# A whole gate unit's slot given back behind its own products, and each expert's case bit taken at its gather

## The chip, the core and the metric

One core of a Trainium2 chip runs the whole program in one launch. The metric is the device time of one execution in microseconds (us); lower is better.

## What is computed

Two layers of a decoder trunk on 256 tokens of width 1024, in fp32. Each layer has a mixer (a gated MLP beside gated linear attention) and a feed-forward part; layer 0's is a dense SwiGLU, layer 1's a mixture of 8 SwiGLU experts of which each token uses 2:

```
logits = t @ w_router
top_val, top_idx = lax.top_k(logits, 2)
gates = sum(one_hot(top_idx) * softmax(top_val))
for e in range(8):
    out = out + gates[:, e:e+1] * ((silu(t @ e_gate[e]) * (t @ e_up[e])) @ e_down[e])
```

The expert weights are 1024 x 3584 (gate, up) and 3584 x 1024 (down), 352 MB in all, and are read once. The change lies in this last stage.

## The kernel before

**Units and slots.** Weights come in units of 1 MB (128 x 2048 fp32). `W`, a `Stream` (lines 127 to 230), holds the list of all units in the order of their use, the plan. A unit passes through slots of SBUF, 18 in this stage. `load` takes a slot and issues the DMA on SP's queue into raw tile r. `converting` takes two more slots and splits r into h (rounded to fp32r, by ACT, line 271) and l (the rest r - h, by DVE, line 272); DVE's l is the last reader of r, whose slot is then given back. PE multiplies with h and l. `drop` gives back l's slot of a unit in an even place, `free` the rest. Slots given back go to the end of the list `idle`, and whoever needs one takes the first. Whoever writes a slot waits for the last reader of what was in it.

**Whole units.** The first unit of every gate block but the very first (line 795, `whole=(0,)`) isn't split: PE takes r as it is, with the input in full fp32 (`self.xw`, line 1050), in twice as many passes of PE; `parts` then holds `(r, None)`. There are 31 such units.

**Order.** The program is written out by Python in the order of PE's products. Before each product step `tick` (line 253) advances the time `W.now` by one, lets side tasks go on, and calls `pump` (line 198): it loads while `len(idle) > 1 + max(0, freed + reserve - split)`, and converts the next unit of the plan where two slots are idle and the unit is due within `lead` ticks (12 here). ACT, DVE and SP each work through their instructions in this order.

**Experts.** An expert's 3584 hidden columns go in groups of 512, 1024, 1024 and 1024 (the last expert in the reverse order). In the main loop (lines 1215 to 1240) a group's gate product (4 units of 1 MB, or 2 for 512 columns), its up product and the down product of the group before follow each other; this is a group's cycle, e.g. 48 ticks. `Expert.product` (line 1035) works by pairs of units. In the narrow case, an expert with at most 64 tokens, the two halves of the input share a pass, and a unit takes two passes; in the wide case it takes three. The third passes, and the last second pass of a pair, run in `last_passes` under a branch (`cases`, line 964: a register holds the expert's bit of a mask; every engine carries the branch). The slots of both units of a pair are given back behind it (`held`). `gated` copies or applies Silu to the gate product (sge), `finish` copies the up product (upe) and, 13 and 17 ticks on, makes the transposed hidden ("hide": PE's folding matmuls with line 1108, ACT line 1110, DVE lines 1111 to 1113). `scatter` adds an expert's output to acc (line 1169). `gather_from_scratch` prepares the next expert's input (exh, exl, xw).

**Registers.** `routing` loads the mask of wide experts into a register of PE, ACT and DVE (line 905) and takes all eight bits out of it at once (line 908).

Numbers of units below are their places in the plan: 290 is ('eu', 5, 2, 1), the second up unit of expert 5's third group; h290, l290 and r290 are its tiles.

Of the kernel before, what the change touches and what calls it, by code (L numbers as in the profile page):

```python
# [39 lines left out]
def trunk(ctx: ExitStack, tc: tile.TileContext, x, w_in, gm_ws, gm_bs, gm_ln_g, gm_ln_b, gla_wa2, gla_ba,  # L40
          gla_norm_g, w_out, ln_mix_g, ln_mix_b, ffn_g, ffn_u, ffn_d, router_w, exp_g, exp_u, exp_d,
          ln_ffn_g, ln_ffn_b, out):
    nc = tc.nc
# [14 lines left out]
    def s2(name, dt=F32, shape=(P, 512)):  # L58
        return act.tile(list(shape), dt, tag="s2", name=name, bufs=6)
# [10 lines left out]
    def psy(name, shape=(P, 512), dt=F32):  # L70
        return ps_y.tile(list(shape), dt, tag="y", name=name)
# [55 lines left out]
    class Stream:  # L127
# [98 lines left out]
        def free(self, key):  # L226
            assert self.index[key] == self.freed, (key, self.index[key], self.freed)
            self.parts.pop(self.freed)
            idle.extend(self.held.pop(self.freed))
            self.freed += 1  # L230
# [596 lines left out]
    def moe(xT, ready, consts):  # L827
# [6 lines left out]
        def logits(tb):  # L834
            pl = psy(f"lg{tb}", (2 * NE, P))
            thin(pl, rw, xT[tb], NE)
            lT = s2(f"lT{tb}", F32, (2 * NE, P))
            nc.scalar.activation(lT, pl, AF.Copy)
            lTs.append(lT)
# [6 lines left out]
        def first_max(src, nm):  # L846
            m = const.tile([P, 2, 1], F32, name=f"m{nm}")
            nc.vector.tensor_reduce(m, src, axis=AX.X, op=ALU.max)
            q = const.tile([P, 2, NE], F32, name=f"q{nm}")
            nc.vector.tensor_tensor(q, src, bc(m), op=ALU.is_equal)  # L850
            nc.vector.tensor_tensor(q, q, pri_b, op=ALU.mult)
            r = const.tile([P, 2, 1], F32, name=f"r{nm}")
            nc.vector.tensor_reduce(r, q, axis=AX.X, op=ALU.max)
            nc.vector.tensor_tensor(q, q, bc(r), op=ALU.is_equal)
            return m, q
# [10 lines left out]
        def routing():  # L866
            yield 2
            logits(0)
            yield 8
            ready.finish()  # L870
            logits(1)
            yield 2
            for tb in range(2):
                nc.tensor.matmul(plt[:, tb, :], lTs[tb], pair, start=True, stop=True)
            nc.vector.tensor_copy(lg, plt)
            m1, oh1 = first_max(lg, "1")
            lg2 = const.tile([P, 2, NE], F32, name="lg2")
            nc.vector.scalar_tensor_tensor(lg2, oh1, -3.0e38, lg, op0=ALU.mult, op1=ALU.add)
            m2, oh2 = first_max(lg2, "2")
            nc.vector.tensor_tensor(sel, oh1, oh2, op=ALU.add)  # L880
            W.pump(1, 100)
            ut = s2("ut")[:, 0:P]
            nc.gpsimd.memset(ut, 1.0)
            nc.gpsimd.affine_select(ut, ut, pattern=[[1, P]], compare_op=ALU.is_ge, fill=0.0, base=-1,
                                    channel_multiplier=-1)
            yield 6

            pr = psy("pr", (P, 2, NE))
            nc.tensor.matmul(pr[:, 0, :], ut, sel[:, 0, :], start=True, stop=True)
            nc.tensor.matmul(pr[:, 1, :], ut, sel[:, 1, :], start=True, stop=False)  # L890
            nc.tensor.matmul(pr[:, 1, :], ones, sel[:, 0, :], start=False, stop=True)
            pc = psy("pc", (P, NE))
            for tb in range(2):
                nc.tensor.matmul(pc, ones, sel[:, tb, :], start=tb == 0, stop=tb == 1)
            nc.vector.scalar_tensor_tensor(rk, pr, 1.0, sel, op0=ALU.add, op1=ALU.mult)
            nc.vector.tensor_scalar(rk, rk, -1.0, None, op0=ALU.add)
            nc.vector.tensor_scalar(small, pc, HALF + 0.5, float(-HALF), op0=ALU.is_lt, op1=ALU.mult)

            bits = const.tile([P, NE], F32, name="bits")
            msum = const.tile([P, 1], F32, name="msum")  # L900
            nc.vector.scalar_tensor_tensor(bits, pc, HALF + 0.5, powers, op0=ALU.is_gt, op1=ALU.mult)
            nc.vector.tensor_reduce(msum, bits, axis=AX.X, op=ALU.add)
            nc.vector.tensor_copy(mask_i, msum)
            experts[0].one_hot()
            mask = nc.values_load(mask_i[0:1, 0:1], engines=[ET.PE, ET.Activation, ET.DVE], min_val=0,
                                  max_val=2 ** NE - 1)
            for e in range(NE):
                experts[e].wide = nc.snap(mask & 2 ** e)
            W.pump(1, 100)
            yield 1  # L910
            yield from experts[0].gather()

            cnt = const.tile([P, 1], F32, name="cnt")
            nc.vector.tensor_reduce(cnt, pc, axis=AX.X, op=ALU.max)
            nc.vector.tensor_copy(cnt_i, cnt)
            W.hold = False
            yield 60

            w12 = const.tile([P, 2, 2], F32, name="w12")
            dl = const.tile([P, 2], F32, name="dl")  # L920
            nc.vector.tensor_tensor(dl, m2[:, :, 0], m1[:, :, 0], op=ALU.subtract)
            nc.gpsimd.tensor_tensor(dl, ecst, dl, op=ALU.pow)
            nc.vector.tensor_scalar(w12[:, 0, :], dl, 1.0, None, op0=ALU.add)
            nc.vector.reciprocal(w12[:, 0, :], w12[:, 0, :])
            nc.vector.tensor_tensor(w12[:, 1, :], dl, w12[:, 0, :], op=ALU.mult)
            for tb in range(2):
                nc.vector.tensor_scalar(gates[:, tb, :], oh1[:, tb, :], w12[:, 0, tb:tb + 1], None, op0=ALU.mult)
                nc.vector.scalar_tensor_tensor(gates[:, tb, :], oh2[:, tb, :], w12[:, 1, tb:tb + 1], gates[:, tb, :],
                                               op0=ALU.mult, op1=ALU.add)
                nc.vector.tensor_scalar(acc[tb], xf[tb], ALPHA, None, op0=ALU.mult)  # L930
# [20 lines left out]
        class Expert:  # L951
# [6 lines left out]

            def __init__(self, nm, rank, gate, fewer=None):
                self.nm, self.rank, self.gate, self.fewer = nm, rank, gate, fewer  # L960
                self.wide = None
                self.hT = {}

            def cases(self, few, many):
# [36 lines left out]
                                         stop=tb == 1)  # L1001

            def gather_from_scratch(self):
                self.one_hot()
                yield 4
                yield from self.gather()
# [28 lines left out]
            def product(self, units, n, nm):  # L1035

                xh, xl = self.x
                nb = n // 512
                p = [psw(f"{nm}{b}") for b in range(nb)]
                kk = 2048 // n  # L1040
                held, rest, last = [], [], []
                for u, ((wh, wl), free, drop) in enumerate(units):
                    held.append(free)
                    for j in range(kk):
                        k = kk * u + j
                        for b in range(nb):
                            s = slice(b * 512, b * 512 + 512)
                            tick()
                            if wl is None:
                                nc.tensor.matmul(p[b], self.xw[:, k, :], wh[:, j, s], start=k == 0, stop=False,  # L1050
                                                 skip_group_check=True)
                                continue
                            nc.tensor.matmul(p[b], xh[:, k, :], wh[:, j, s], start=k == 0, stop=False,  # L1053
                                             skip_group_check=True)
                            rest.append((p[b], xl[:, k, :], wh[:, j, s], False))
                            second = p[b], xh[:, k, :], wl[:, j, s], k == KT - 1
                            if k == KT - 1 or (u % 2, j, b) == (1, kk - 1, nb - 1):
                                last.append(second)
                            else:
                                nc.tensor.matmul(*second[0:3], start=False, stop=False, skip_group_check=True)  # L1060
                    if u % 2 == 0:
                        drop()
                    if u % 2 and (nb > 1 or u == 1):
                        self.last_passes(rest, last)
                        for free in held:
                            free()
                        held, rest, last = [], [], []
                return p
# [104 lines left out]
        def stream(keys):  # L1173
            for key in keys:
                yield W.get(key), lambda key=key: W.free(key), lambda key=key: W.drop(key)

        experts = [Expert(str(e), lambda tb, e=e: rk[:, tb, e:e + 1], lambda tb, e=e: gates[:, tb, e:e + 1],
                          small[:, e:e + 1]) for e in range(NE)]
# [222 lines left out]
```

## Time and profile before

| | |
|---|---|
| three runs | 1342.43, 1343.06, 1344.02 us; median 1343.06 |
| the profiled execution | 1342.48 us |
| its span, first to last instruction | 1340.8 us |
| granted TensorE clock, mean over the span | 0.996 |
| DMA moved | 426.35 MB, mean 318 GB/s |

The profile is of one execution. Busy time is that of an engine's instructions; "<-" names whose semaphore ended an idle stretch; a name with q (DVEq, SPq) is that engine's sequencer, and PEld is the weight load of PE. In the timeline equal instructions that follow each other stand in one row with their count, and the bracket is the idle time before the first. The MoE stage takes the time from some 430 us to the end; its first expert's products begin earlier, beside the routing.

### The profile page before, as it was taken

Reading aid. Unit: us, or ns where it says so; the run is one execution under the profiler, and the core shown is the slowest. Engines: PE = TensorE matmul, PEld = TensorE weight load, DVE = VectorE, ACT = ScalarE, POOL = GpSimd, SP = SyncE. Lnnn points to the kernel's source line nnn. Section 1 sums busy time; section 2 is a strip of 40 time slices with the busy share of each in tenths; the row PEclk is TensorE's granted clock in tenths of the full one; section 3 lists DMA queues with packets and bytes.
Section 4 is the critical chain, followed back from the end, with each engine's and each line's share of the span. In section 5 each row is a group of like instructions: output and inputs, shape, how many; then the busy total and the mean of one; then the engine's idle time right before and its main releaser. Section 6 shows DMA issues by size and latency. Waiting matters only on the chain. (4 is left out here: it accounts for less than half of the span.)

```text
span 1340.8 us, 16964 instructions
## 1 busy us (share of the span) xinstructions
PE 1296.5 (97%) x6113; PEld 1024.0 (76%) x6113; DVE 1068.5 (80%) x965; ACT 839.0 (63%) x702; POOL 37.7 (3%) x79
## 2 busy tenths in 40 slices
PE   8999999999998999999999999999999999999996
PEld 7878888888887788777778877776776776777774
DVE  6687544476684887898888789899899989989997
ACT  5653444346342666687756667776777777877783
POOL 1012000000110000000000000000000000000000
PEclk9999999999999999999999999999999999999998
DMA  9636656543484598999999899999999999999993
GB/s 343 256 126 205 240 188 204 203 157 132 159 301 162 222 365 321 392 370 380 408 368 369 320 384 370 389 408 412 408 389 408 409 393 410 407 400 403 412 407 118
DMA packets 118766, 426.35 MB, mean 318 GB/s; under 512 B 8089, under 2 KB 10722, under 8 KB 104578
## 3 DMA queue, kind: packets, MB, share of 16 engines
q1 hardware_dynamic: 117218, 420.61, 81.0%
q0 software_dynamic: 1440, 4.33, 1.1%
q8 instruction: 64, 1.05, 0.3%
q14 instruction: 44, 0.36, 0.1%
HBM read 423.86 MB, written 1.05 MB: 317 GB/s over the span
## 5 line engine op out<-in xcount | busy, mean ns | idle before, releaser
L272 DVE TENSOR_TENSOR l<-r,h 128x2048 fp32r<-128x2048 f32 (+2 forms) x373 | 833.3, 2249 | 134.0 <-ACT h L271 117.6
L271 ACT ACTIVATE h<-r 128x2048 fp32r<-128x2048 f32 (+2 forms) x373 | 685.0, 1881 | 124.1 <-PE bank L1032 39.1
L1137 PE MATMUL bank<-h,che 128*128 128x512 f32 x440 | 174.4, 396 | 0.0
L1053 PE MATMUL eu<-h,exh 128*128 128x512 f32 x440 | 167.5, 389 | 0.0
L1144 PE MATMUL bank<-l,che 128*128 128x512 f32 x377 | 153.3, 407 | 7.0 <-DVEq L969 3.5
L1060 PE MATMUL eu<-l,exh 128*128 128x512 f32 x361 | 141.0, 391 | 0.3 <-DVE l L272 0.3
L1053 PE MATMUL eg<-h,exh 128*128 128x512 f32 x316 | 128.2, 418 | 0.0
L1050 PE MATMUL eg<-r,xw 128*128 128x512 f32 x248 | 114.5, 595 | 0.0
L1144 PEld LDWEIGHTS bank<-l,che 128*128 128x128 f32 x377 | 70.8, 188 | 41.9 <-DVE l L272 17.1
L1053 PEld LDWEIGHTS eu<-h,exh 128*128 128x128 f32 x440 | 82.6, 188 | 16.9
L1137 PEld LDWEIGHTS bank<-h,che 128*128 128x128 f32 x440 | 82.8, 188 | 15.2
L1060 PE MATMUL eg<-l,exh 128*128 128x512 f32 x237 | 92.7, 391 | 0.1
L1060 PEld LDWEIGHTS eu<-l,exh 128*128 128x128 f32 x361 | 67.8, 188 | 15.9 <-DVE l L272 2.1
L1050 PEld LDWEIGHTS eg<-r,xw 128*128 128x128 f32 x248 | 45.2, 190 | 39.6 <-issue 37.8
L266 PE MATMUL f<-h,xhm 128*128 128x512 f32 (+1 forms) x192 | 72.2, 376 | 0.0
L267 PE MATMUL f<-l,xhm 128*128 128x512 f32 (+1 forms) x192 | 71.4, 372 | 0.0
L268 PE MATMUL f<-h,xlm 128*128 128x512 f32 (+1 forms) x192 | 71.4, 372 | 0.0
L1053 PEld LDWEIGHTS eg<-h,exh 128*128 128x128 f32 x316 | 59.5, 188 | 15.4 <-issue 4.1
L1110 ACT ACTIVATE hide<-bank 128x256 f32<-128x256 f32 x42 | 16.1, 384 | 71.7 <-PE bank L1108 71.7
L1060 PEld LDWEIGHTS eg<-l,exh 128*128 128x128 f32 x237 | 44.6, 188 | 12.7 <-issue 3.8
L1075 ACT ACTIVATE sge<-eg 128x512 f32<-128x512 f32 x55 | 30.2, 595 | 36.4 <-PE eg L1032 36.3
L1108 PEld LDWEIGHTS bank<-fold,sge 128*128 128x128 f32 x336 | 46.0, 196 | 5.2 <-issue 2.4
(354 smaller groups left out, 1803.3 us busy)
## 6 DMA issues: line engine op xcount, KB each, us to landing
r<-in_exp_w_gate SPq DMA_DIRECT2D x112, 1024.0 KB, 11.1
r<-in_exp_w_up SPq DMA_DIRECT2D x112, 1024.0 KB, 7.5
r<-in_exp_w_down SPq DMA_DIRECT2D x110, 1024.0 KB, 11.6
r<-in_w_in SPq DMA_DIRECT2D x17, 1024.0 KB, 8.5
r<-in_ffn_w_gate SPq DMA_DIRECT2D x11, 1024.0 KB, 6.9
r<-in_ffn_w_up SPq DMA_DIRECT2D x11, 1024.0 KB, 5.3
r<-in_ffn_w_down SPq DMA_DIRECT2D x11, 1024.0 KB, 4.9
r<-in_w_out SPq DMA_DIRECT2D x8, 1024.0 KB, 9.2
```

The lines of the kernel that those rows point to most:

```text
L266: nc.tensor.matmul(ps, xh, wh, start=start, stop=False)
L267: nc.tensor.matmul(ps, xh, wl, start=False, stop=False)
L268: nc.tensor.matmul(ps, xl, wh, start=False, stop=stop)
L271: nc.scalar.activation(dst_h, src, AF.Copy)
L272: nc.vector.tensor_tensor(dst_l, src, dst_h.bitcast(F32), op=ALU.subtract)
L1050: nc.tensor.matmul(p[b], self.xw[:, k, :], wh[:, j, s], start=k == 0, stop=False, skip_group_check=True)
L1053: nc.tensor.matmul(p[b], xh[:, k, :], wh[:, j, s], start=k == 0, stop=False, skip_group_check=True)
L1060: nc.tensor.matmul(*second[0:3], start=False, stop=False, skip_group_check=True)
L1075: nc.scalar.activation(o, i, f)
L1108: nc.tensor.matmul(tp[:, j, i * HALF:i * HALF + HALF], hidden_columns(t, j), fold, start=True, stop=True)
L1137: nc.tensor.matmul(y, ch[:, k, :], wh[:, j, s], start=first and u + j == 0, stop=False, skip_group_check=True)
L1144: nc.tensor.matmul(y, ch[:, k, :], wl[:, j, s], start=False, stop=False, skip_group_check=True)
```

## The change

Three things change. In `product`, a whole unit's slot is no longer held to the end of its pair; `free` is called right behind its own four product steps. The eight bits are no longer taken out at once: `experts[e].bit` is a function, called for expert 0 in `routing` and for the others at the beginning of `gather_from_scratch`. The operator loop behind the last expert, which runs only if an expert has more than 128 tokens, has no bit.

```diff
--- before.py
+++ after.py
@@ -905,7 +905,8 @@
             mask = nc.values_load(mask_i[0:1, 0:1], engines=[ET.PE, ET.Activation, ET.DVE], min_val=0,
                                   max_val=2 ** NE - 1)
             for e in range(NE):
-                experts[e].wide = nc.snap(mask & 2 ** e)
+                experts[e].bit = lambda e=e: nc.snap(mask & 2 ** e)
+            experts[0].wide = experts[0].bit()
             W.pump(1, 100)
             yield 1
             yield from experts[0].gather()
@@ -958,7 +959,7 @@
 
             def __init__(self, nm, rank, gate, fewer=None):
                 self.nm, self.rank, self.gate, self.fewer = nm, rank, gate, fewer
-                self.wide = None
+                self.wide = self.bit = None
                 self.hT = {}
 
             def cases(self, few, many):
@@ -1001,6 +1002,8 @@
                                          stop=tb == 1)
 
             def gather_from_scratch(self):
+                if self.bit is not None:
+                    self.wide = self.bit()
                 self.one_hot()
                 yield 4
                 yield from self.gather()
@@ -1040,7 +1043,8 @@
                 kk = 2048 // n
                 held, rest, last = [], [], []
                 for u, ((wh, wl), free, drop) in enumerate(units):
-                    held.append(free)
+                    if wl is not None:
+                        held.append(free)
                     for j in range(kk):
                         k = kk * u + j
                         for b in range(nb):
@@ -1058,7 +1062,9 @@
                                 last.append(second)
                             else:
                                 nc.tensor.matmul(*second[0:3], start=False, stop=False, skip_group_check=True)
-                    if u % 2 == 0:
+                    if wl is None:
+                        free()
+                    elif u % 2 == 0:
                         drop()
                     if u % 2 and (nb > 1 or u == 1):
                         self.last_passes(rest, last)
```

What this does to the order of instructions is shown at three places. Rows are as the built programs have them: line, operation, out<-in, shape, and the semaphores waited for (DVE_49 is DVE's, PE_49 PE's, Activation_49 ACT's, DMAHW those of DMAs). A number behind an underscore is the tile's, and differs between programs without meaning.

ACT in expert 5's last group, at the end of the first gate pair (297 and 298); exh6 is the next expert's input. Before:

```order
L271 ACTIVATE h301_9327<-r301_9102 128x2048 [waits DMAHW6_49]
L969 COMPARE_AND_BRANCH
L271 ACTIVATE exh6_9310<-bank3_3526 128x512 [waits PE_49]
L969 UNCONDITIONAL_BRANCH
L991 ACTIVATE exh6_9310<-bank3_3526 128x4x64 [waits PE_49]
L969 UNCONDITIONAL_BRANCH
L969 COMPARE_AND_BRANCH
L969 UNCONDITIONAL_BRANCH x2
L271 ACTIVATE h302_9361<-r302_9122 128x2048 [waits DMAHW7_49,DMAHW2_49]
L271 ACTIVATE h303_9371<-r303_9140 128x2048 [waits DMAHW0_49,PE_49]
```

With the change:

```order
L271 ACTIVATE h301_9317<-r301_9082 128x2048 [waits DMAHW6_49]
L970 COMPARE_AND_BRANCH
L271 ACTIVATE exh6_9300<-bank3_3456 128x512 [waits PE_49]
L970 UNCONDITIONAL_BRANCH
L992 ACTIVATE exh6_9300<-bank3_3456 128x4x64 [waits PE_49]
L970 UNCONDITIONAL_BRANCH
L271 ACTIVATE h302_9341<-r302_9102 128x2048 [waits DMAHW7_49,DVE_49]
L970 COMPARE_AND_BRANCH
L970 UNCONDITIONAL_BRANCH x2
L271 ACTIVATE h303_9361<-r303_9120 128x2048 [waits DMAHW0_49,PE_49]
```

h302 now stands ahead of the branch of the pair's last passes, and waits for DVE instead of DMAs long landed.

ACT between experts 4 and 5, around the first gate pair of expert 5 (267 and 268), whose product is eg500 and its copy sge500. Before:

```order
L271 ACTIVATE h271_8580<-r271_8386 128x2048 [waits DMAHW0_49,DVE_49]
L969 COMPARE_AND_BRANCH
L969 UNCONDITIONAL_BRANCH x2
L969 COMPARE_AND_BRANCH
L1075 ACTIVATE sge500_8599<-eg500_8548 128x512 [waits PE_49]
L969 UNCONDITIONAL_BRANCH
L1075 ACTIVATE sge500_8599<-eg500_8548 128x512 [waits PE_49]
L969 UNCONDITIONAL_BRANCH
L271 ACTIVATE h272_8606<-r272_8406 128x2048 [waits DMAHW4_49,DMAHW1_49]
L271 ACTIVATE h273_8616<-r273_8424 128x2048 [waits DMAHW2_49,DVE_49]
```

With the change:

```order
L271 ACTIVATE h271_8560<-r271_8366 128x2048 [waits DMAHW0_49,DVE_49]
L271 ACTIVATE h272_8571<-r272_8386 128x2048 [waits DMAHW1_49,DVE_49]
L970 COMPARE_AND_BRANCH
L970 UNCONDITIONAL_BRANCH x2
L970 COMPARE_AND_BRANCH
L1081 ACTIVATE sge500_8583<-eg500_8528 128x512 [waits PE_49]
L970 UNCONDITIONAL_BRANCH
L1081 ACTIVATE sge500_8583<-eg500_8528 128x512 [waits PE_49]
L970 UNCONDITIONAL_BRANCH
L271 ACTIVATE h273_8596<-r273_8404 128x2048 [waits DMAHW2_49]
```

h272 now stands directly behind h271, ahead of the two branches and of sge500, and waits for DVE; h273 no longer does.

ACT in expert 5's third group, around the first gate pair (285 and 286); hide510 and hide511 are the two halves of the hidden of the group before. Before:

```order
L1110 ACTIVATE hide510_8980<-bank3_3526 128x256 [waits PE_49]
L969 UNCONDITIONAL_BRANCH
L969 COMPARE_AND_BRANCH
L969 UNCONDITIONAL_BRANCH x2
L969 COMPARE_AND_BRANCH
L271 ACTIVATE che511_9014<-bank2_3525 128x512 [waits PE_49]
L969 UNCONDITIONAL_BRANCH
L1110 ACTIVATE hide511_9016<-bank2_3525 128x256 [waits PE_49]
L969 UNCONDITIONAL_BRANCH
L271 ACTIVATE h290_9038<-r290_8842 128x2048 [waits DMAHW6_49,DMAHW3_49]
L271 ACTIVATE h291_9048<-r291_8860 128x2048 [waits DMAHW4_49,DVE_49]
```

With the change:

```order
L1116 ACTIVATE hide510_8960<-bank3_3456 128x256 [waits PE_49]
L970 UNCONDITIONAL_BRANCH
L271 ACTIVATE h290_8986<-r290_8822 128x2048 [waits DMAHW3_49,DVE_49]
L970 COMPARE_AND_BRANCH
L970 UNCONDITIONAL_BRANCH x2
L970 COMPARE_AND_BRANCH
L271 ACTIVATE che511_8998<-bank2_3455 128x512 [waits PE_49]
L970 UNCONDITIONAL_BRANCH
L1116 ACTIVATE hide511_9000<-bank2_3455 128x256 [waits PE_49]
L970 UNCONDITIONAL_BRANCH
L271 ACTIVATE h291_9028<-r291_8840 128x2048 [waits DMAHW4_49]
```

h290 now stands ahead of the second hide. DVE's l302, l272 and l290 move in the same way. In the whole MoE stage 29 conversions move up by one tick like these, one more (unit 69, at the start) by four, and 31 calls of `free` by four. On SP no load is issued at another tick; 29 loads (298, 310 and so on) take the slot of another raw tile, that of the moved unit in place of that of the unit before it.

## Rows read from the trace of the kernel before

**Rows 1.** Page, part 1: busy us, share of the span, instructions by engine.

```profile
PE 1296.5 (97%) x6113; PEld 1024.0 (76%) x6113; DVE 1068.5 (80%) x965; ACT 839.0 (63%) x702; POOL 37.7 (3%) x79
```

**Rows 2.** Windows: us, busy us (PE, PEld, DVE, ACT, POOL), PEclk, DMA share, GB/s.

```profile
460.00:820.00 360.00, 352.81 (x1586) 275.77 (x1586) 303.34 (x215) 243.84 (x185) 0.69 (x1) 1.00 0.94 367
...
820.00:1300.00 480.00, 463.74 (x2166) 355.81 (x2165) 440.41 (x319) 362.70 (x288) 0.00 (x0) 1.00 1.01 404
```

**Rows 3.** Windows of line 1117 (wide transposes): PE, PEld, then as above.

```profile
675.00:775.00 100.00, 3.78 (x24) 3.80 (x24) 1.00 0.90 351
...
795.00:1330.00 535.00, 0.00 (x0) 0.00 (x0) 1.00 0.98 390
```

**Rows 4.** Tile r, 820 to 1300: count, ns min/median/max; DMA to landing.

```profile
L271 ACT ACTIVATE h<-r x170: 1890/1915/1950, 818.4 to 1295.9; 128x2048 fp32r<-128x2048 f32 x170
...
L272 DVE TENSOR_TENSOR l<-r,h x170: 2277/2291/2294, 818.6 to 1297.8; 128x2048 fp32r<-128x2048 f32 x170
...
DMA to landing us min/median/max: 5.0/11.0/17.1
```

**Rows 5.** Waits, 820 to 1300: us in total, times, longest.

```profile
ACT h L271 <- PE eg L1050: 7.2, 4, 1.8
...
DVE l L272 <- ACT h L271: 23.1, 30, 2.5
...
PEld bank L1144 <- DVE l L272: 12.8, 25, 0.7
...
PEld bank L1144 <- DVEq L969: 9.7, 15, 0.7
```

**Rows 6.** Timeline, start of the stage: start us, us, engine, what, [idle before].

```profile
440.75 3.72 ACT L271 ACTIVATE h<-r 128x2048 fp32r<-128x2048 f32 x2 [2.93 <-DVE l L272]
...
442.70 6.88 DVE L272 TENSOR_TENSOR l<-r,h 128x2048 fp32r<-128x2048 f32 x3 [1.98 <-ACT h L271]
```

**Rows 7.** Line 908 on PE's sequencer; the timeline row behind it.

```profile
L908 PEldq ALU_OP  x8: 32/32/42, 415.8 to 417.0; - x8
...
417.22 0.19 PEld L266 LDWEIGHTS e<-h,xhm 128*128 128x128 f32 x1 [3.19 <-issue]
```

**Rows 8.** Timeline, spot C of expert 5: ACT, DVE, SP.

```profile
1084.77 1.09 ACT L1075 ACTIVATE sge<-eg 128x512 f32<-128x512 f32 x2 [0.81 <-PE eg L1032]
...
1085.74 7.33 ACT L271 ACTIVATE h<-r 128x2048 fp32r<-128x2048 f32 x4
...
1080.12 2.29 DVE L272 TENSOR_TENSOR l<-r,h 128x2048 fp32r<-128x2048 f32 x1 [2.46 <-ACT h L271]
...
1082.66 4.67 DVE L272 TENSOR_TENSOR l<-r,h 128x2048 fp32r<-128x2048 f32 x2
...
1087.69 9.26 DVE L272 TENSOR_TENSOR l<-r,h 128x2048 fp32r<-128x2048 f32 x4 [0.36 <-ACT h L271]
...
1071.38 11.43 SPq L169 DMA_DIRECT2D r<-in_exp_w_gate  x2
```

**Rows 9.** Timeline of DVE, spot D between experts 4 and 5.

```profile
997.25 4.67 DVE L272 TENSOR_TENSOR l<-r,h 128x2048 fp32r<-128x2048 f32 x2 [0.27 <-ACT h L271]
...
1002.80 2.29 DVE L272 TENSOR_TENSOR l<-r,h 128x2048 fp32r<-128x2048 f32 x1 [0.87 <-ACT h L271]
...
1005.54 2.29 DVE L272 TENSOR_TENSOR l<-r,h 128x2048 fp32r<-128x2048 f32 x1 [0.45 <-DVE l L272]
```

**Rows 10.** Timeline of DVE, spot B of expert 5.

```profile
1039.50 6.88 DVE L272 TENSOR_TENSOR l<-r,h 128x2048 fp32r<-128x2048 f32 x3
...
1049.94 6.88 DVE L272 TENSOR_TENSOR l<-r,h 128x2048 fp32r<-128x2048 f32 x3 [0.59 <-ACT h L271]
```

**Rows 11.** Timeline of DVE, spot E, expert 7's first group.

```profile
1215.78 9.26 DVE L272 TENSOR_TENSOR l<-r,h 128x2048 fp32r<-128x2048 f32 x4 [0.27 <-ACT h L271]
...
1225.22 6.88 DVE L272 TENSOR_TENSOR l<-r,h 128x2048 fp32r<-128x2048 f32 x3 [0.18 <-ACT h L271]
```

**Rows 12.** Timeline of DVE, spot A of expert 5.

```profile
1029.87 4.67 DVE L272 TENSOR_TENSOR l<-r,h 128x2048 fp32r<-128x2048 f32 x2 [0.87 <-ACT h L271]
```

## The prediction

> **What bounds the kernel now.** I read the page first: PE is busy 97% of the span, DVE 80% [rows 1]. A share over the whole span hides the stages, so next come the windows. From 820 to 1300 us the DMA share is 1.01 at 404 GB/s, PE 464 and DVE 440 of 480 us; from 460 to 820 the DMA share is 0.94 and PE is busy 353 of 360 [rows 2]. The same view, kept to line 1117, tells which experts take the wide case (more than 64 tokens, three passes): 24 transposes from 675 to 775 us, none after 795 [rows 3]; by the same view expert 0 is the other wide one, so experts 1 and 3 to 7 run the narrow case.
>
> Three engines near full leave open which one sets the pace, and the waits decide it. Look at who waits for whom from 820 to 1300: PE waits 40 times for the l half of a down unit (L1144 behind DVE l, or behind DVE's branch), 22.5 us together; DVE waits 30 times for an ACT h, 23.1 us [rows 5]. No row of that answer has ACT or DVE waiting for a landing of in_exp data. A load takes 5.0 to 17.1 us to land, 11.0 at the middle [rows 4], and it lands in time. So in the narrow experts the pace is a ring: PE frees slots, ACT and DVE convert the next units in program order, and PE stalls at the first down units until DVE has finished theirs. The DMA queue is full, but nobody waits for it. In the wide experts PE has a third pass and DVE runs ahead.
>
> **What the change moves.** It reads as "a slot comes back four ticks sooner, so a load starts sooner". The order says otherwise. The pump's test compares free slots with freed + reserve - split; one slot more and one freed more leave it where it was, and not one load is issued at an earlier tick. What moves, 29 times in the MoE stage and once a little differently, is one conversion, that of the second unit behind a gate pair (I call it c): it goes from just behind the pair's last passes to just ahead of them, one tick. And the slots change hands: h of c now goes into the slot that raw c-1 leaves, l of c into the whole unit's; the load that used to take raw c-1's slot takes raw c's.
>
> This has one price and one gain. The gain: l of c no longer waits for PE's pair. The price: h of c can't start before DVE has finished l of c-1, since DVE reads that raw slot; until now ACT made h of c while DVE made l of c-1. The kernel has this wait once already, at the start of the MoE stage: ACT starts at 440.75 "<-DVE l", DVE starts its l at 442.70 and has sat idle 1.98 us for it [rows 6]. That is the price I take; it is an h of 1.9 us and the step to DVE [rows 4, 6]. What it costs in time depends on what DVE had at that spot before, so I go by spots, on one narrow expert each.
>
> Spot C (second up unit of an expert's last group; experts 1 and 3 to 6). l of 301 runs 1080.12 + 2.29 = 1082.41, l of 302 starts at 1082.66 [rows 8]. With the change: 1082.41 + 1.98 = 1084.39, 1.7 us later. On ACT h 303 follows (ends about 1086.3), the two sge copies of 1.09 in all, then h 304: its l starts at about 1089.3 where it started at 1087.69 [rows 8]. That l is the first of four in one stretch of 9.26 us that ends at the down units for which PE stalls, so PE is late by the same **1.6 us**, and all that hangs on PE's frees with it. 5 x 1.6 = 8.0.
>
> Spot D (second down unit of an expert's last group, converted beside the next expert's first gate pair: units 104, 188, 230, 272, 314, each with a narrow expert next). l of 270 and 271 end at 997.25 + 4.67 = 1001.92; l of 272 starts at 1002.80 and 273 at 1005.54, with 0.87 and 0.45 us idle before them [rows 9]. With the change 272 starts at 1003.90; ACT goes on with an sge copy of 0.55 (half of the two at C [rows 8]) and h 273, so l 273 starts at about 1006.35: **0.8 us** late, at a unit for which PE waits. 5 x 0.8 = 4.0. Unit 146, the sixth, has wide expert 2 next, where PE has three passes to go through: 0.
>
> Spot E (expert 7, whose large groups come first: units 356 and 380). Seven l follow each other with a gap of 0.18 us, 9.26 and 6.88 us [rows 11]; nothing lies in the hole, and PE waits at the end of the row: **2.0 us** each, 4.0.
>
> Spot B (third group of experts 1 and 3 to 6). Today h of 290 stands behind the second hide, and DVE idles 0.59 before l of 290 at 1049.94; the l before ended at 1039.50 + 6.88 = 1046.38 [rows 10]. With the change it starts at 1046.38 + 1.98 = 1048.36, the second hide's three operations come behind it, and l of 291 starts 0.5 us earlier than today. 5 x **-0.5** = -2.5.
>
> Spot A (first large group; 7 units, 112 the first): DVE has two accumulations to fill the hole, and two units on, at 1029.87, it waits 0.87 for an h that hangs on PE's gate product [rows 12]; 0. If that cover were gone, an A would cost some 0.7. Spots B and C in experts 0 and 2 lie in the wide case, where PE has work: 0. The first group of the stage (unit 69) only swaps which of two conversions waits for DVE: +0.3. The last group's swap (unit 394) lies ahead of idle DVE: 0.
>
> The registers: the eight bits took eight ALU_OPs on PE's sequencer, begun from 415.8 to 417.0, 0.17 us apart, and PE's idle of 3.19 us ended behind them at 417.22 [rows 7]. Seven go to later gathers: 7 x 0.17 = **1.2 us** less there. Later each stands alone beside a branch that PE's queue covers: 0; on DVE and ACT it lies in idle time at the gather: 0.
>
> The late loads: 29 loads wait for l of c where they waited for l of c-1. At C the pair of issues spans 1071.38 + 11.43 [rows 8], the second going out as l of 301 ends; it will go out at about 1086.7, 4.2 us later. Against a middle of 11.0 us from issue to landing [rows 4] that eats into the queue and seldom empties it: 0, and the rivals hold the other case. How the trace and a rule differ here: by the trace no conversion waits for data. The Trainium skill (Perfetto Trace Analysis, Identifying the Most-Contended Engine) has DMA judged by HBM utilization and the highest engine improved first; 404 over its 358 GB/s is 113%, so by that rule DMA would be the bound, the holes on DVE would be free, and the sum would be that of the second case below.
>
> **Sum**: 8.0 + 4.0 + 4.0 - 2.5 + 0.3 - 1.2 = +12.6 us. Against the profiled execution's own 1342.48 us that is **1355.1**; that execution lies 0.6 below the median of the three runs, 1343.06. Bounds of the new hole: if each of the twelve paying spots costs half of mine, because PE's slack takes in the rest, the sum is 8.0 - 3.4 = +4.6 (1347.1); if each costs the whole 1.98, it is 23.8 - 3.4 = +20.4 (1362.9). I take the sum by spots, since rows 8 to 11 are these spots themselves.
>
> **Rivals.**
> Second case, no change, 0.09: the DMA queue sets the pace after 820 us. For it: share 1.01, 404 GB/s [rows 2]. Against it: the missing waits for data, the 40 stalls behind DVE [rows 5]. Then DVE's holes vanish in DMA time and only the registers and unit 69 stay: 1342.48 - 1.2 + 0.3 = 1341.6.
>
> Third case, faster, 0.06: the added wait finds DVE's l always done, because ACT comes late to h of c anyway. Its place is ACT's queue; it decides where ACT today reaches c over 2.3 us (an l [rows 4]) after c-1's h. For it: ACT waits 7.2 us in 4 waits for the whole unit's products [rows 5], a wait that goes. Against it: at C and E the h follow each other. Then B and the registers remain: 1342.48 - 2.5 - 1.2 = 1338.8. The Trainium skill (Perfetto Trace Analysis, Optimization Strategy) says that a gap that keeps repeating can mean too little SBUF for the next tile; by that rule, too, a slot that comes sooner helps. The row at A speaks against it: the l there starts behind other work of DVE without a gap of its own.
>
> Fourth case, slower still, 0.05: at the five C spots the queue does run dry. The load before went out at 1071.4 [rows 8] and lands 11.0 to 17.1 us later [rows 4], by 1088.5 at the latest; the late one goes out at 1086.7 and lands 5.0 us later or more, at 1091.7, where the 2.6 us that 1 MB takes at 404 GB/s would have it at 1091.1: a hole of 0.6 us, or of several where the load before came at the middle time. With 2 us each, waited for by ACT, it is 1355.1 + 5 x 2 = 1365. It decides only where a landing comes after ACT is ready for it, and the waits show none today.
>
> That the change doesn't do what it says is no case of its own: it does, and the slot it frees is used for something else.
>
> **How the numbers follow.** The forecast has 0.80. About 0.2% (2.7 us) is what a measurement of this kernel can tell from no change. Faster 0.06 and same 0.09 are the third and second case; slower 0.85 the rest. The range, 1346 to 1361, takes in the forecast down to its lower bound and up to 1.9 us short of the upper one; the second and third case, 0.15 together, and the fourth lie outside.
>
> **What would show it.** Right: after 820 us ACT h "<-DVE l" appears some 20 times, DVE l "<-ACT h" grows from 23.1 us [rows 5] to about 45, PE's stalls at L1144 grow from 22.5 by some 8, DVE's busy time stays, and GB/s falls by about 1%. At the start PE's idle of 3.19 shrinks to about 2. Wrong: if DVE's waits grow and PE's do not, there was slack in the ring that I didn't see; if ACT waits for landings, the DMA was the bound.

## The result, and the profile after

Slower. The changed kernel takes 1353.75 us, median of four runs (1352.47 to 1354.91), beside 1342.74 for the kernel before (four runs, 1342.19 to 1344.02): ratio 1.0078, interval 1.0064 to 1.0092, that is 8.6 to 12.4 us. The profiled execution took 1352.47 us, with a span of 1350.8; against the profiled one of before, 1342.48, it is 9.99 us longer. The forecast was 1355.1.

The busy times stay, the span grows. Part 1 of the page of the changed kernel (before: [rows 1]), and its windows with the columns of [rows 2]:

```profile
PE 1301.7 (96%) x6113; PEld 1020.3 (76%) x6113; DVE 1068.2 (79%) x965; ACT 838.5 (62%) x702; POOL 36.8 (3%) x79
```

```profile
460.00:820.00 360.00, 351.43 (x1574) 273.24 (x1573) 300.98 (x214) 243.30 (x184) 0.70 (x1) 1.00 0.93 364
820.00:1300.00 480.00, 460.00 (x2120) 347.31 (x2119) 430.59 (x315) 354.30 (x282) 0.00 (x0) 1.00 1.00 398
```

DVE and ACT do the same work (1068.2 for 1068.5, 838.5 for 839.0). In the same 480 us DVE gets 9.8 us less of it done and the DMAs move 398 GB/s for 404. What holds DVE up stands in the waits from 820 to 1300 (before: [rows 5]):

```profile
ACT h L271 <- DVE l L272: 52.3, 17, 5.4
...
DVE l L272 <- ACT h L271: 34.3, 32, 2.5
...
PEld bank L1150 <- DVE l L272: 14.0, 26, 0.7
PEld bank L1150 <- DVEq L970: 10.3, 16, 0.7
PEld eu L1064 <- DVE l L272: 9.5, 18, 0.8
...
DVE l L272 <- PE eg L1035: 2.0, 1, 2.0
```

Of the kernel before, for the row of the up units:

```profile
PEld eu L1060 <- DVE l L272: 0.9, 4, 0.2
```

The row of ACT h behind DVE's l was not there before. DVE's waits for an h grow from 23.1 to 34.3 us. PE's stalls for the l of a down unit (L1150, L1144 before) hardly grow, from 22.5 to 24.3; its stalls for the l of an up unit (L1064, L1060 before) grow to 9.5 us from 0.9 in 4. Expert 5's way through the groups shows it spot by spot, on DVE's timeline (columns as in [rows 6]):

```profile
999.92 4.68 DVE L272 TENSOR_TENSOR l<-r,h 128x2048 fp32r<-128x2048 f32 x2 [0.27 <-ACT h L271]
1006.58 4.58 DVE L272 TENSOR_TENSOR l<-r,h 128x2048 fp32r<-128x2048 f32 x2 [1.98 <-ACT h L271]
...
1011.43 2.29 DVE L272 TENSOR_TENSOR l<-r,h 128x2048 fp32r<-128x2048 f32 x1 [0.27 <-DVEq L970]
...
1033.20 6.88 DVE L272 TENSOR_TENSOR l<-r,h 128x2048 fp32r<-128x2048 f32 x3 [0.29 <-ACT h L271]
...
1051.69 2.29 DVE L272 TENSOR_TENSOR l<-r,h 128x2048 fp32r<-128x2048 f32 x1 [0.86 <-ACT h L271]
...
1083.08 2.29 DVE L272 TENSOR_TENSOR l<-r,h 128x2048 fp32r<-128x2048 f32 x1 [2.46 <-ACT h L271]
...
1087.36 13.84 DVE L272 TENSOR_TENSOR l<-r,h 128x2048 fp32r<-128x2048 f32 x6 [1.65 <-ACT h L271]
1101.47 6.88 DVE L272 TENSOR_TENSOR l<-r,h 128x2048 fp32r<-128x2048 f32 x3 [0.27 <-DVEq L970]
```

The start of a unit's l here, less its start before, is how late DVE runs. Ahead of spot D (l 270) 999.92 - 997.25 [rows 9] = 2.67. The hole of 1.98 stands at 1006.58, the length that [rows 6] had shown at the start of the stage. Behind D it is 1011.43 - 1008.10 = 3.33 (the row of the kernel before stands below), and behind A 1033.20 - 1029.87 [rows 12] = 3.33 again. Behind B 1083.08 - 1080.12 [rows 8] = 2.96. Behind C, where the hole shows as 1.65 idle and an exh beside it, 1101.47 less the second of these rows of the kernel before

```profile
1008.10 6.87 DVE L272 TENSOR_TENSOR l<-r,h 128x2048 fp32r<-128x2048 f32 x3 [0.27 <-DVEq L969]
...
1097.22 6.88 DVE L272 TENSOR_TENSOR l<-r,h 128x2048 fp32r<-128x2048 f32 x3 [0.27 <-DVEq L969]
```

gives 4.25. So D cost 0.66, A nothing, B gave back 0.37, C cost 1.29. The same sum over all spots, from the starts of all l in the two traces, is in the table under the experiments. At E, expert 7's first group, the l behind the spot starts 1242.70 - 1234.75 = 7.95 late and the one ahead of it 1221.94 - 1215.78 [rows 11] = 6.16: 1.79 for this hole.

```profile
1221.94 4.67 DVE L272 TENSOR_TENSOR l<-r,h 128x2048 fp32r<-128x2048 f32 x2 [0.26 <-ACT h L271]
1228.60 13.84 DVE L272 TENSOR_TENSOR l<-r,h 128x2048 fp32r<-128x2048 f32 x6 [1.98 <-ACT h L271]
1242.70 4.49 DVE L272 TENSOR_TENSOR l<-r,h 128x2048 fp32r<-128x2048 f32 x2 [0.27 <-DVEq L970]
```

```profile
1234.75 6.88 DVE L272 TENSOR_TENSOR l<-r,h 128x2048 fp32r<-128x2048 f32 x3 [0.27 <-DVEq L969]
```

The first three rows are the changed kernel's, the last is of the kernel before.

The other end of a hole is on ACT (changed kernel, spot C; before: [rows 8]): h of 302 waits 2.09 us for DVE's l of 301. In the kernel before, whose row stands last here, it followed an exh without a gap.

```profile
1085.41 3.72 ACT L271 ACTIVATE h<-r 128x2048 fp32r<-128x2048 f32 x2 [2.09 <-DVE l L272]
1089.03 1.06 ACT L1081 ACTIVATE sge<-eg 128x512 f32<-128x512 f32 x2
1089.98 7.32 ACT L271 ACTIVATE h<-r 128x2048 fp32r<-128x2048 f32 x4
```

```profile
1080.25 3.72 ACT L271 ACTIVATE h<-r 128x2048 fp32r<-128x2048 f32 x2
```

And PE, on the weight loads of the same stretch, in the changed kernel and then in the one before:

```profile
1089.70 0.19 PEld L1064 LDWEIGHTS eu<-l,exh 128*128 128x128 f32 x1 [0.20 <-DVE l L272]
1091.91 0.19 PEld L1064 LDWEIGHTS eu<-l,exh 128*128 128x128 f32 x1 [0.51 <-DVE l L272]
1094.28 0.19 PEld L1064 LDWEIGHTS eu<-l,exh 128*128 128x128 f32 x1 [0.69 <-DVE l L272]
1096.67 0.19 PEld L1150 LDWEIGHTS bank<-l,che 128*128 128x128 f32 x1 [0.70 <-DVE l L272]
```

```profile
1092.42 0.19 PEld L1144 LDWEIGHTS bank<-l,che 128*128 128x128 f32 x1 [0.47 <-DVE l L272]
1094.62 0.19 PEld L1144 LDWEIGHTS bank<-l,che 128*128 128x128 f32 x1 [0.51 <-DVE l L272]
```

Before, PE caught up with DVE at the down units; now it does so three units earlier, at the up units that come right behind the hole, and from there both go at DVE's pace.

At the start, PE's idle of 3.19 us [rows 7] is 1.90. The clock behind it differs too. The 16 gather products of L1000 (L1001 now), before and in the changed kernel:

```profile
418.43 3.39 PE L1000 MATMUL gx<-oh,xin 128*128 128x128 f32 x16
```

```profile
415.47 0.19 PEld L266 LDWEIGHTS e<-h,xhm 128*128 128x128 f32 x1 [1.90 <-issue]
...
416.48 1.95 PE L1001 MATMUL gx<-oh,xin 128*128 128x128 f32 x16
```

Before, the granted clock in the windows 418 to 420 and 420 to 422 us was 0.51 and 0.64 of 2.4 GHz, so behind the idle it was at its lower level of 1.2 GHz for nearly all of the one and part of the other; in this execution of the changed kernel it stayed at 1.00, worth 3.39 - 1.95 = 1.44 us.

### The profile page after: what moved, and what is told of

It reads as the page before. It is cut to its first block, busy times and chain, and to the rows that moved or that the text cites. A ratio compares the mean times of both kernels' runs of the same rounds, so it can differ in the third digit from the quotient of the medians.

```text
span 1350.8 us, 16921 instructions
## 1 busy us (share of the span) xinstructions
PE 1301.7 (96%) x6113; PEld 1020.3 (76%) x6113; DVE 1068.2 (79%) x965; ACT 838.5 (62%) x702; POOL 36.8 (3%) x79
## 5 line engine op out<-in xcount | busy, mean ns | idle before, releaser
L1150 PE MATMUL bank<-l,che 128*128 128x512 f32 x377 | 154.2, 409 | 9.2 <-DVEq L970 3.8
L1064 PE MATMUL eu<-l,exh 128*128 128x512 f32 x361 | 143.0, 396 | 3.9 <-DVE l L272 3.3
L1150 PEld LDWEIGHTS bank<-l,che 128*128 128x128 f32 x377 | 70.8, 188 | 46.7 <-DVE l L272 21.0
L1064 PE MATMUL eg<-l,exh 128*128 128x512 f32 x237 | 92.7, 391 | 0.1
L1064 PEld LDWEIGHTS eu<-l,exh 128*128 128x128 f32 x361 | 67.7, 188 | 26.2 <-DVE l L272 12.8
L1064 PEld LDWEIGHTS eg<-l,exh 128*128 128x128 f32 x237 | 44.6, 188 | 12.7 <-issue 3.8
L1114 PE MATMUL bank<-fold,upe 128*128 128x64 f32 x336 | 46.4, 281 | 0.0
```

The lines of the kernel that those rows point to most:

```text
L1114: nc.tensor.matmul(tp[:, j, i * HALF:i * HALF + HALF], hidden_columns(t, j), fold, start=True, stop=True)
L1150: nc.tensor.matmul(y, ch[:, k, :], wl[:, j, s], start=False, stop=False, skip_group_check=True)
```

## The experiments

The theory is the prediction's: h of c, now in the slot of raw c-1, waits for DVE, and the hole that this leaves on DVE costs the time. The rivals: the 29 loads that go out later, the earlier place in the order, the register part. "Spots" are those of the prediction.

**The register part alone.** The kernel before with the first three hunks of the diff: `bit` in place of `wide` in `routing`, in `__init__`, and called in `gather_from_scratch`.

> The kernel before with the register part alone: one bit in routing, seven at the later gathers; slots as before. Prediction's own term: 7 x 0.17 = 1.2 us less, 1341.5. Theory from the profile of the changed kernel: PE's idle stretch behind the routing shrinks from 3.19 to about 1.9 us, and the granted clock, which fell to 0.51 in the 2 us from 418 on, stays at 1.00, so that the 16 gather products behind it take 1.95 us where they took 3.39; together 2.7 us less, about 1340.0. Rival: the fallen clock was an accident of that one execution; then the idle shrinks, the clock falls or not regardless, and the time is 1341.5.

Measured: 1341.40 us (11 runs) beside 1342.74 (15 runs), ratio 0.9991 (0.9982 to 1.0000): 1.3 us less, by the interval from nothing to 2.4. That agrees with the prediction's term, which is this run's rival; the 2.7 of the theory did not come. Its idle is 1.87 us, and yet its clock fell, as the window from 418 to 420 us (PEclk is the third number from the end) and the gather products show:

```profile
418.00:420.00 2.00, 2.00 (x11) 2.00 (x11) 0.00 (x0) 0.00 (x0) 0.00 (x0) 0.50 0.00 0
```

```profile
417.31 3.57 PE L1001 MATMUL gx<-oh,xin 128*128 128x128 f32 x16
```

So the 1.44 us of the changed kernel's first profile are not a sure part of the change. Whether the seven later bits cost something, the changed kernel answers: from unit 69 to 394 it loses 13.30 us to the kernel before, and the next run, which has none of them, 13.15, so they cost some 0.2 there at most.

**The slot part alone.** The kernel before with the last two hunks.

> The kernel before with the early free of whole units alone, all eight bits in routing. Theory (the wait of h of c for l of c-1 costs the time, spot by spot): as the changed kernel without its gain at the start, 1353.75 + 2.7 = 1356.5, with ACT h waiting for DVE l some 17 times after 820 us. If the register part is worth 1.2 us only: 1355.0. If it were the register part that costs (a bit behind a branch at each gather): 1342 to 1345.

Measured: 1355.86, ratio 1.0096 (1.0081 to 1.0112): 13.1 us more. It has the same 17 waits of ACT, 52.3 us. The early free is the whole loss; the changed kernel's 11.0 is this less what the start gives back. The 2.1 between them is more than the 1.3 of the registers; the clock that stayed up may be the rest, which is not shown.

**The same order and ticks, other hands.** The changed kernel, with the whole unit's slot at the front of the list:

```diff
         def free(self, key):
...
-            idle.extend(self.held.pop(self.freed))
+            if self.freed in self.whole:
+                idle[0:0] = self.held.pop(self.freed)
+            else:
+                idle.extend(self.held.pop(self.freed))
```

> The changed kernel, but a whole unit's slot goes to the front of the list instead of the end. h of c then takes the whole unit's slot and l of c that of raw c-1; order and ticks, and the late load into raw c's slot, stay as in the changed kernel. Theory (the new wait between ACT and DVE is the cost): the holes at C, D and E vanish, B's -0.4 x 5 and the -2.7 of the registers stay: 1342.7 - 4.7 = 1338.0, at most 1342. Rival, the 29 late loads cost the time: as slow as the changed kernel, 1350 to 1354. Rival, the earlier place in the order costs it (work behind it on ACT and DVE held up): also 1350 to 1354, with no ACT h waiting for DVE l.

Measured: 1336.99, ratio 0.9953 (0.9940 to 0.9967): 5.75 us less than before, faster than both kernels; it is called the third kernel below. Conversions stand where the changed kernel has them, and the loads still take raw c's slot; only h and l have exchanged slots. At spot C its DVE has no hole:

```profile
1075.43 2.29 DVE L275 TENSOR_TENSOR l<-r,h 128x2048 fp32r<-128x2048 f32 x1 [2.46 <-ACT h L274]
...
1077.97 4.48 DVE L275 TENSOR_TENSOR l<-r,h 128x2048 fp32r<-128x2048 f32 x2
```

ACT's waits for DVE's l from 820 to 1300 are down to one of 0.6 us. Its gain beside the registers: 0.7 at the first group, 0.4 at each of four B, 0.4 to 0.7 at three D. By the Trainium skill (Perfetto Trace Analysis, Optimization Strategy) a gap that keeps repeating can mean too little SBUF for the next tile. This kernel agrees in part: a slot four ticks sooner brought DVE forward by 1.6 us at B and 1.5 at D. The changed kernel, with as many slots at the same ticks, made new gaps instead.

**The same wait in the order of before.** That diff on the kernel before: the whole unit's slot comes back at the pair's end, as before, but in front. The load takes it, h of c takes raw c-1's, l of c is where it was.

> The kernel before in its own order, whole units freed at the pair's end as before, but their slot goes to the front of the list. The load then takes the whole unit's slot (no later than before), h of c that of raw c-1, l of c stays as it was. So it has the wait of h of c for l of c-1, without the late loads, without the earlier place and without the registers. Theory (that wait is the cost): the terms of C, D and E as the trace of the changed kernel has them, 6.6 + 4.3 + 3.8 = 14.7, no gain at B: 1342.7 + 14.7 = 1357.4, range 1353 to 1360. Rival, late loads or the place in the order: 1342 to 1344.

Measured: 1357.07, ratio 1.0106 (1.0090 to 1.0121): 14.3 us more; this is the fourth kernel. The wait does it without the late loads, the earlier place and the registers. Its loads go out earlier than before: the two gate loads at C end 11.43 us [rows 8] behind their start there, 6.86 here.

```profile
1077.51 6.86 SPq L169 DMA_DIRECT2D r<-in_exp_w_gate  x2
```

In the waits from 820 to 1300:

```profile
ACT h L274 <- DVE l L275: 38.3, 13, 5.4
DVE l L275 <- ACT h L274: 34.2, 30, 2.5
```

**Spot by spot.** The kernel before with the early free at one kind of spot, chosen by the group (here C):

```diff
                 for u, ((wh, wl), free, drop) in enumerate(units):
-                    held.append(free)
+                    key = next(k for k, i in W.index.items() if i == W.freed) if wl is None else None
+                    early = wl is None and key[1] < 7 and key[2] == 3
+                    if not early:
+                        held.append(free)
...
-                    if u % 2 == 0:
+                    if early:
+                        free()
+                    elif u % 2 == 0:
                         drop()
```

> The kernel before, whole units freed early at the C spots alone (first gate pair of the last group of experts 0 to 6), slot to the end of the list as in the changed kernel; all eight bits in routing. Theory (each spot pays its own hole and the terms add): the five narrow C of 1.3 us each, as the traces of the changed kernel and of e2_slot have them, 6.6 in all: 1342.7 + 6.6 = 1349.3. The prediction's 1.6 each: 1350.7. Rival, the spots share slack, so that one kind alone is taken in by the next group: under 1346.

Measured: 1349.92 beside 1342.56 (9 runs), ratio 1.0053 (1.0039 to 1.0066), 7.4 us more (5.2 to 8.9); 6.5 by the trace.

> The same for the two E spots of the last expert alone (units 356 and 380). Theory: 2 x 1.9 = 3.8, 1346.5; the prediction's 2 x 2.0: 1346.7. Rival, as for C: under 1344.

Measured: 1347.33, ratio 1.0036 (1.0023 to 1.0050), 4.8 us more (3.1 to 6.7); 3.6 by the trace.

> The kernel before, whole units freed early at the B spots alone (first gate pair of the third group of experts 0 to 6), slot to the end of the list; all eight bits in routing. Theory: the five narrow B give back 0.4 each as the traces of the changed kernel, e2_slot and e8_again have them (the prediction: 0.5), the two wide ones nothing: 1342.6 - 2.0 = 1340.6. Rival, the gain at B exists only where a C before it has made DVE late: 1342.6, no change.

Measured: 1341.44 beside 1343.04 (24 runs), ratio 0.9987 (0.9978 to 0.9996), 1.6 us less; 2.0 by the trace, and the gain is there without any late C before it.

> The same at the D spots alone (second down unit of an expert's last group, experts 0 to 5). Theory: five times 0.6 to 1.0, 4.3 in all by the traces (the prediction: 4.0): 1346.9. Rival, slack at the next group's start takes it in: under 1344.5.

Measured: 1347.21, ratio 1.0030 (1.0019 to 1.0040), 4.2 us more; 4.3 by the trace.

> The same at the A spots alone (first gate pair of an expert's first large group, experts 1 to 6, and unit 368). Theory, and the prediction: DVE has other work for the hole, 0: 1342.6, within 0.8. Rival, the cover is only there while DVE is late from C and D: 7 x 0.7 = 4.9, 1347.5.

Measured: 1343.02, ratio 0.9997 (0.9988 to 1.0006): nothing, by the trace as well, although ACT waits there for DVE (4 times, 21.1 us, from 820 to 1300):

```profile
DVE l L272 <- ACT h L271: 23.5, 34, 2.5
ACT h L271 <- DVE l L272: 21.1, 4, 5.4
```

DVE's waits stay at 23.5 (23.1 before [rows 5]): ACT has the time to spare at these four places, and its waits cost nothing.

| term, us | prediction | changed kernel, by its trace | alone, by its trace |
|---|---|---|---|
| C, 5 narrow | +8.0 | +6.9 | +6.5 |
| D, 5 | +4.0 | +4.3 | +4.3 |
| E, 2 | +4.0 | +3.6 | +3.6 |
| B, 5 narrow | -2.5 | -2.0 | -2.0 |
| A, 7; and the wide C, B, D | 0 | +0.1 | +0.1 |
| first group (unit 69) | +0.3 | +0.5 | +0.5 (slot part) |
| PE's idle at the registers | -1.2 | -1.3 | -1.3 |
| clock behind it | 0 | -1.4 | 0 |
| work ahead of the MoE stage | 0 | -0.5 | |
| not assigned | | -0.3 | |
| sum | +12.6 | +9.9 | |

A term by a trace is how much later the next group's l start less how late the l ahead of the spot started, summed over its spots; kernels that agree in a spot's slots agree in its term to 0.02 us at most spots. Two exceptions: of the changed kernel's C at expert 3, 0.36 is gone again by unit 228, which accounts for the -0.3 not assigned; and in the kernel with the register part alone, whose slots are those of before, DVE's lateness steps up by 0.36 and 0.38 at units 128 and 300 and down by 0.35 at 273. So one step of 0.4 proves nothing by itself. B's stands at all five narrow spots in each of four profiled executions: both of the changed kernel, the slot part's, and the one with B alone.

**The late loads.** The third kernel, with one more case (only this is shown; the rest of its diff is the third kernel's): the two slots of a pair's second unit go to the front too, so that the load takes one of them and l of the next unit raw c's.

```diff
+            elif self.freed - 1 in self.whole:
+                idle[0:0] = self.held.pop(self.freed)
             else:
                 idle.extend(self.held.pop(self.freed))
```

> e3_front, and behind a pair with a whole unit the second unit's two slots go to the front of the list too: the load takes the h slot of the pair's second unit, which PE frees, in place of raw c's, which DVE frees later; h of the next unit takes its l slot, and l of the next unit raw c's (DVE's own). So the 29 loads are no longer late. Theory (late loads cost nothing): as e3_front, 1337.0, within 0.7. Rival, they cost something that e3_front's gains hide: 1333 to 1336. If the new hands make a wait that I don't see: over 1338.

Measured: 1337.99, ratio 0.9963 (0.9949 to 0.9976): 1.0 us more than the third kernel's 1336.99, 0.3 over what was expected, with overlapping intervals. At the same spot its loads end 3.7 us sooner behind the same start:

```profile
1066.45 14.21 SPq L169 DMA_DIRECT2D r<-in_exp_w_gate  x2
```

```profile
1066.41 10.53 SPq L169 DMA_DIRECT2D r<-in_exp_w_gate  x2
```

The first row is the third kernel's, the second this one's. Nothing comes of it: from unit 66 to 394 the third kernel gains 3.4 us on the kernel before and this one 2.9, so the late loads cost nothing that these runs can show.

**The changed kernel again.**

> The changed kernel once more, for the clock behind the routing. In its first profile the granted clock stayed at 1.00 there, in e1_bits and e3_front, with the same idle of 1.9 us, it fell to 0.50. Theory (an accident of that execution): it falls here as well, the 16 gather products take 3.4 to 3.6 us, and the profiled execution lies at 1353.7 or over, with the median at 1353.8. Rival, the changed kernel keeps the clock up: 1.95 us, and a median of 1352.5.

Measured: 1354.25 (five runs), ratio 1.0082 (1.0069 to 1.0096). The clock stayed up here too, as the rival had it, and yet the profiled execution took 1354.98 us, as the theory had it: half of each expectation. What differs between the two profiled executions of the changed kernel lies ahead of the stage. The first l of the experts' weights (unit 61) came 0.46 us earlier than in the kernel before in the one, 1.93 us later in the other; from that l to unit 394's, two units from the end, both lose the same, 10.35 and 10.41 us.

## Why the prediction was right, and where it was off

**What bounds.** Right. The ring of PE's frees, DVE and ACT sets the pace, not the DMA queue. The second case fell with the fourth kernel, which sends its loads earlier and loses 14.3 us. Nor were 404 GB/s the most that the queue could move, as the third kernel's window shows:

```profile
820.00:1300.00 480.00, 465.51 (x2185) 358.93 (x2184) 441.88 (x323) 364.91 (x289) 0.00 (x0) 1.00 1.02 407
```

By the Trainium skill (Perfetto Trace Analysis, Identifying the Most-Contended Engine) the DMA, with the highest utilization, was the engine to optimize first. Here the measurement speaks against the rule: slots dealt out otherwise between ACT and DVE cost 14.3 us in one kernel and, with the registers, gained 5.75 in another, and the run that gave the queue its work sooner, the one with the early loads, gained nothing.

**The price.** Right: 1.98 us of DVE at D and E, the length of [rows 6]. The third case (the wait always finds l done) fell with the 17 waits of ACT. The third kernel, where one such wait of 0.6 us is left, came out faster, at 1336.99.

**The spots.** Right in sign, and within 0.5 us for each kind but C, the term that was mis-sized: 1.6 each in the prediction, 1.24 to 1.63 in the changed kernel (6.9 in all for 8.0). The step that failed is the way along ACT: h 303 "(ends about 1086.3), the two sge copies of 1.09 in all, then h 304". It puts durations end to end, and rows of one engine overlap: in [rows 8] the copies end at 1084.77 + 1.09 = 1085.86, and the h behind them starts at 1085.74. The shorter way is DVE's own idle: a hole costs its length less the gaps that it swallows before PE next stalls. The sums that follow are those of one spot each. C: 1.65 - 0.36 [rows 8] = 1.29, measured 1.29 at expert 5. D: 1.98 - 0.87 - 0.45 [rows 9] = 0.66, measured 0.66 (up to 1.02 at the others). E: 1.98 - 0.18 [rows 11] = 1.80, measured 1.79 and 1.81; the prediction had left out the 0.18. B: 0.86 now, before 0.59 [rows 10] and this gap ahead of the second hide, 1.24 together, so -0.38, measured -0.4:

```profile
1048.14 0.42 DVE L1111 TENSOR_TENSOR hide<-bank,hide 128x256 f32<-128x256 f32 x1 [0.65 <-ACT hide L1110]
```

How near the total came is in part luck. From unit 69 to 394 the spots sum to 13.8 in the prediction and to 13.3 in the trace, because C and E, set too high, and B, D and the first group, set too low, cancel in part; and the profiled execution is 1.9 us shorter by the clock and by work ahead of the stage, which no term of the prediction has.

**The registers.** Right: PE's idle shrank by 1.3 for 1.2; the time of that part alone agrees, with an interval that reaches from nothing to 2.4. The clock was not in the sum; both profiled executions of the changed kernel have its 1.4 us, and from unit 61 on they would be some 11.8 us longer than before without it (10.35 + 1.44, an estimate).

**The late loads.** Right: 4.2 us late in the prediction, 15.76 - 11.43 [rows 8] = 4.3 in this row of the changed kernel, and 0 of cost.

```profile
1074.30 15.76 SPq L169 DMA_DIRECT2D r<-in_exp_w_gate  x2
```

The landing times hardly change (5.0, 11.0 and 17.1 before [rows 4]), and the waits from 820 to 1300 hold none for in_exp data: the fourth case did not come.

```profile
DMA to landing us min/median/max: 4.9/11.0/18.5
```

**What was to be seen.** Two marks were off. DVE's waits for h were to reach 45 and reached 34.3, because the gaps that a hole swallows leave that row, and because one hole of 2.0 stands in another row, behind PE's eg. PE's stalls were to grow at L1144 by 8; they grew by 1.8 there and by 8.6 at L1064, the up units right behind the hole.

## What to carry to other kernels

A buffer given back earlier is worth what its next taker makes of it: look up who last read the buffer that each following writer gets, for the early slot may push another engine's slot onto the writer, and with it a wait. A hole on the engine that sets the pace costs its length less the idle that it swallows up to the next stall of its consumer; which gaps lie there can be read from the trace before the change. Here one line decides the sign: the slot that PE frees must go to ACT, and the one that DVE itself leaves to DVE (1336.99 us, where the slot at the list's end gave 1353.75).

## What the runs showed that was not expected

**The clock after a short idle.** In the eight profiled executions with PE idle 3.16 to 3.19 us behind the routing the granted clock fell to its lower level of 1.2 GHz (0.50 to 0.57 in the lowest window of 2 us); in the five with 1.87 to 1.90 it fell in two and stayed at 1.00 in three. Each fall made the first 16 gather products take 2.5 to 3.6 us for 1.95. What decides it at the shorter idle stays open.

**Executions differ ahead of the stage, hardly in it.** The first l of the experts' weights came between 1.16 us earlier and 1.93 us later than in the kernel before, over twelve profiled executions, with no edit that could move it. Behind it most spots repeat to 0.02 us, so that one trace against another gives a term of 0.4 us, where several spots of a kind repeat it, which the times of whole runs, with intervals of 2 us and more, do not.
